# First modulations by single feature tile, with fill matmuls and earlier weight splits, and the last additions behind the products

## The chip, the cores and the metric

The kernel runs on one core of a Trainium2 chip. The metric is the device time of one execution in microseconds (us). The engines are named as in the profile: PE is TensorE's matmul, PEld its weight load, DVE is VectorE, ACT is ScalarE, POOL is GpSimd, SP is SyncE, which issues most transfers. Each engine works through its own queue in the order in which the built program lists it.

## The reference, cut to what matters

Two layers of a diffusion trunk run for 128 context tokens and 256 latent tokens that share all weights, so T = 384 columns. The model width is 1024, that is 8 feature tiles of 128. Each layer is half SwiGLU FFN, token mixing, half FFN, each with RMSNorm and a shift, scale and gate that come from a condition vector:

```python
def _modulation(cond, w, b):
    m = jax.nn.silu(cond) @ w + b
    return jnp.split(m[:, None, :], N_MOD, axis=-1)

def _ada_norm(x, g, shift, scale):
    return _rms(x, g) * (1 + scale) + shift

def _half_ffn(x, shift, scale, gate, g, w1, w3, w2):
    h = _ada_norm(x, g, shift, scale)
    f = (jax.nn.silu(h @ w1) * (h @ w3)) @ w2
    return x + 0.5 * gate * f
```

Nothing can be multiplied in the first FFN before shift and scale of the first sub-layer are known. After the second layer's last FFN only a final RMSNorm follows.

## The kernel before

**Products.** Activations lie with features on the 128 partitions and tokens in columns. Every product is made of three in reduced precision: a value is split into a high part (`hh`, `whi`, cast on ACT, L211) and the rest (`hl`, `wlo`, subtracted on DVE, L212 and L233). `mm3x` (L352 to L354) issues the three: `whi` with `hh`, `whi` with `hl`, `wlo` with `hh`. A *unit* is one of 22 column blocks of `w1` and `w3` of an FFN; it has 8 feature tiles times 2 halves times 3 products = 48 matmuls. The norm's factor is applied after the products, so products can start before the norm is known; its mean is a matmul with ones (L206), whose sum of squares comes from ACT (squares, L200) and POOL (additions, L201).

**The start ("boot").** The modulations of the first sub-layer are computed on PE. The weights come in quarters `q` of two feature tiles each, and each quarter in two halves of 1 MB over the contraction. `sums(q)` multiplies them with the condition (`cs`) in four column strips of 32 of the array, one strip for each pair of shift or scale and feature tile, and DVE copies the result (L954). `apply(q)` transposes it on PE (L958), adds the bias (L960), makes the scale (L123) and the shift's two parts, and then `feed` multiplies x: `hh` on ACT (L232) and `hl` on DVE (L233), each in a context and a latent piece. `begin(ft, ks)` issues the six products of each named feature tile for unit 0 or 1. `load_to` and `split_to` load and split FFN weights (`raw`, `whi`, `wlo`) in the order of a list; three raw buffers and four of each split half are there. PE's order in this block is the order of the code; that of the other engines is chosen by the scheduler. x comes in pairs of feature tiles on the same SP queue.

**The end.** `project_out` computes the second FFN product in four slices `s` of two feature tiles (`m`), and `finish` adds it to x with the gate (L400), takes the square for the next norm and multiplies by the next factor (`feed`). For the last slice of the whole kernel (`apart`) all products of `m` = 0 come before those of `m` = 1, and `finish` of `m` = 0 stands between the two. `Last.finish` (L265) then makes the mean of each token group from two terms, the POOL sum of tiles 0 to 6 and the squares of tile 7, and `put` scales and stores.

Of the kernel before, what the change touches and what calls it, by code (L numbers as in the profile page):

```python
# [43 lines left out]
def trunk(ctx, tc, a):  # L44
# [347 lines left out]
    def project_out(nk, parts, l, v, nxt, name, shared=False, order=None):  # L392
# [14 lines left out]
        for s in range(4):  # L407
            acc = two_banks(f"{name}_acc{s}")
            for k0 in range(0, nk, KD):
# [5 lines left out]
                for m, k in [(m, k) for m in range(2) for k in ks] if apart else [(m, k) for k in ks for m in range(2)]:  # L415
# [5 lines left out]
                    if apart and last:  # L421
                        finish(acc, s, m)
                pump()
            if not apart:
                for m in range(2):
                    finish(acc, s, m)
# [491 lines left out]
    with tc.tile_pool(name="boot", bufs=1) as bp, tc.manual_schedule(engines={mybir.EngineType.PE}):  # L918
        raw_mod, rows = {}, {}

        def load(q):
            nc.sync.dma_start(x[:, 2 * q : 2 * q + 2], a["xT"][:, 2 * q : 2 * q + 2])
            for half in range(2):
                raw_mod[q, half] = bp.tile([P, 4, 512], F32, name=f"raw_mod0_{q}{half}")
                nc.sync.dma_start(raw_mod[q, half], a["modw0"][q, half].rearrange("p (k c) -> p k c", k=4))

        load(0)
        load_to(2)
        for q in range(1, 4):
            load(q)  # L930
        load_to(3)
        units = []

# [10 lines left out]
        def sums(q):  # L944
            acc = one_bank(f"mod0_{q}")[:, :P]
            for half in range(2):
                for k in range(4):
                    for j in range(4):
# [4 lines left out]
            rows[q] = bp.tile([P, P], F32, name=f"modrow0_{q}")  # L953
            dve.tensor_copy(rows[q], acc)  # L954

        def apply(q):
            pt = one_bank(f"modt0_{q}")
            pe.transpose(pt[:, :P], rows[q], ident)  # L958
            for v in range(2):
                dve.tensor_tensor(  # L960
                    mods[0][v][:, 2 * q : 2 * q + 2],
                    pt[:, :P].rearrange("p (v d c) -> p v d c", v=2, d=2)[:, v, :, 0:2],
                    pcol("modb")[:, v * KD + 2 * q : v * KD + 2 * q + 2].unsqueeze(2).broadcast_to([P, 2, 2]),
                    op=ALU.add,
                )
            mod_fix(0, 1, 2 * q, 2 * q + 2)
            feed.shifts(2 * q, 2 * q + 2)
            for d in (2 * q, 2 * q + 1):
                feed.feed(d)
# [183 lines left out]
```

## Time and profile before

| | |
|---|---|
| time, median of 3 runs (lowest to highest) | 1434.32 us (1434.02 to 1434.58) |
| profiled execution: time, span | 1434.01 us, 1432.2 us |
| PE busy, share of the span | 1405.7 us, 98% |
| DVE busy | 1088.3 us, 76% |
| ACT busy | 599.2 us, 42% |
| POOL busy | 123.8 us, 9% |
| bytes moved | 245.26 MB, 171 GB/s over the span |

The span is from the first to the last instruction; the time of the profiled execution is 1.8 us more. Matmuls overlap in their pipeline: one product of 384 columns is listed with 0.34 us, though the next one starts 0.17 or 0.18 us after it, so intervals between starts tell the pace and not the listed length. Idle time of PE is what counts most, and it lies in the first 30 us and the last 15.

### The profile page before, as it was taken

To read this page: it belongs to the slowest core of one execution; us is meant where nothing else is said; L and a number is where in the kernel's file an instruction comes from. 1 tells how busy PE (TensorE), PEld (TensorE's weight loads), DVE (VectorE), ACT (ScalarE), POOL (GpSimd) and SP (SyncE) were. 2 spreads that over 40 slices of the span, in tenths; PEclk is the share of its full clock that TensorE was granted. 3 is DMA by queue.
4 is the path that set the end of the run, shared out by engine and by line. 5 is a ranking of instruction groups with operands and counts; after the bars stand their busy time and mean duration, and the time that the engine had idled before them with its cause. 6 is when DMAs were issued, how large, how long until landed. Compare 5 with 4: busy or idle time off the path is not lost.

```text
span 1432.2 us, 21543 instructions
## 1 busy us (share of the span) xinstructions
PE 1405.7 (98%) x8512; PEld 1367.7 (95%) x8512; DVE 1088.3 (76%) x1829; ACT 599.2 (42%) x981; POOL 123.8 (9%) x97
## 2 busy tenths in 40 slices
PE   6999999999999999999999999999999999999996
PEld 5999999999889999999999999999976999999996
DVE  3899989879876888888869988885687676666433
ACT  4544343435344444343344434333357443444332
POOL 2000000102102000000100000010146200000001
PEclk9999999999999999999999999999999999999999
DMA  9666666563414456656646655665420244333331
GB/s 394 253 215 210 213 198 246 204 223 108 155 45 148 143 195 208 203 178 226 214 162 208 213 209 183 204 213 181 146 89 2 103 141 154 136 130 130 121 103 44
DMA packets 48515, 245.26 MB, mean 171 GB/s; under 512 B 5376, under 2 KB 9856, under 8 KB 29088
## 3 DMA queue, kind: packets, MB, share of 16 engines
q1 hardware_dynamic: 44560, 240.80, 48.3%
q10 hardware_dynamic: 3856, 3.10, 0.7%
q8 instruction: 66, 1.08, 0.3%
q14 instruction: 33, 0.27, 0.1%
HBM read 241.79 MB, written 2.10 MB: 170 GB/s over the span
## 4 chain that ended last, share of the span: by engine, by line
PE 96%; DMA 2%; DVE 1%; ACT 0%; issue 0%; SPq 0%; DVEq 0%; ACTq 0%
PE ffn_p L352 17%; PE ffn_p L354 17%; PE ffn_p L353 17%; PE ffn_acc L345 9%; PE ffn_acc L346 9%; PE ffn_acc L347 9%; DMA raw_mod<-in_modw 2%; PE out_acc L345 2%; PE out_acc L347 2%; PE out_acc L346 2%; PE av L870 1%; PE attn L797 1%; PE attn L352 1%; PE attn L848 1%; PE attn L353 1%; PE attn L354 1%
## 5 line engine op out<-in xcount | busy, mean ns | idle before, releaser
L211 ACT CAST whi<-raw 128x1024 fp32r<-128x1024 f32 (+2 forms) x317 | 324.6, 1027 | 606.5 <-PE ffn_p L353 285.5
L212 DVE TENSOR_TENSOR wlo<-raw,whi 128x1024 fp32r<-128x1024 f32 (+2 forms) x317 | 378.6, 1197 | 164.2 <-ACT whi L211 163.4
L352 PE MATMUL ffn_p<-hh,whi 128*128 128x388 f32 x1408 | 478.4, 340 | 3.0 <-ACT whi L211 3.0
L354 PE MATMUL ffn_p<-hh,wlo 128*128 128x386 f32 x1408 | 475.1, 337 | 0.3 <-DVE wlo L212 0.2
L353 PE MATMUL ffn_p<-hl,whi 128*128 128x384 f32 x1408 | 472.5, 336 | 0.0
L149 DVE SCALAR_TENSOR_TENSOR junk<-modw,cb 128x1024 f32<-128x1024 f32 x256 | 314.4, 1228 | 2.1
L352 PEld LDWEIGHTS ffn_p<-hh,whi 128*128 128x128 f32 x1408 | 265.3, 188 | 4.3 <-ACT whi L211 3.3
L354 PEld LDWEIGHTS ffn_p<-hh,wlo 128*128 128x128 f32 x1408 | 265.9, 189 | 1.5 <-DVE wlo L212 1.5
L353 PEld LDWEIGHTS ffn_p<-hl,whi 128*128 128x128 f32 x1408 | 264.8, 188 | 0.5
L345 PE MATMUL ffn_acc<-gh_ffn,whi 128*128 128x384 f32 x704 | 237.0, 337 | 0.8 <-DVE x L400 0.8
L347 PE MATMUL ffn_acc<-gh_ffn,wlo 128*128 128x384 f32 x704 | 236.9, 337 | 0.0
L346 PE MATMUL ffn_acc<-gl_ffn,whi 128*128 128x384 f32 x704 | 236.9, 336 | 0.0
L201 POOL TENSOR_TENSOR ssq_n<-ssq_n,sq_n 128x384 f32<-128x384 f32 x42 | 59.1, 1408 | 891.6 <-ACT sq_n L200 867.3
L345 PEld LDWEIGHTS ffn_acc<-gh_ffn,whi 128*128 128x128 f32 x704 | 132.8, 189 | 1.2 <-DVE x L400 1.2
L347 PEld LDWEIGHTS ffn_acc<-gh_ffn,wlo 128*128 128x128 f32 x704 | 132.7, 189 | 0.0
L346 PEld LDWEIGHTS ffn_acc<-gl_ffn,whi 128*128 128x128 f32 x704 | 132.7, 189 | 0.0
L438 DVE TENSOR_TENSOR ffn_e<-ffn_p,r_n 128x768 f32<-128x768 f32 x88 | 84.0, 955 | 49.0 <-PE ffn_p L354 48.9
L83 ACT ACTIVATE ffn_e<-ffn_e,ffn_wb 128x128 f32<-128x128 f32 (+1 forms) x176 | 70.2, 448 | 55.3 <-DVE ffn_wb L372 55.0
L212 DVE TENSOR_TENSOR gl_ffn<-ffn_e,gh_ffn 128x384 fp32r<-128x384 f32 x88 | 49.0, 557 | 36.4 <-ACT gh_ffn L211 36.2
L211 ACT CAST gh_ffn<-ffn_e 128x384 fp32r<-128x384 f32 x88 | 44.9, 512 | 58.8 <-DVE ffn_e L442 58.3
L442 DVE SCALAR_TENSOR_TENSOR ffn_e<-ffn_e,ffn_wb 128x128 f32<-128x128 f32 (+1 forms) x176 | 65.0, 412 | 0.0
L233 DVE SCALAR_TENSOR_TENSOR hl<-x,mods,hh 128x128 fp32r<-128x128 f32 (+1 forms) x96 | 57.2, 638 | 2.1 <-ACT hh L232 1.3
(260 smaller groups left out, 1251.5 us busy)
## 6 DMA issues: line engine op xcount, KB each, us to landing
raw<-in_w SPq DMA_DIRECT2D x120, 1024.0 KB, 4.8
modw<-in_modw SPq DMA_DIRECT2D x128, 512.0 KB, 3.4
raw<-in_w SPq DMA_DIRECT2D x16, 768.0 KB, 4.9
raw_mod<-in_modw SPq DMA_DIRECT2D x8, 1024.0 KB, 15.7
raw<-in_w_in SPq DMA_DIRECT2D x8, 1024.0 KB, 5.0
raw<-in_w_out SPq DMA_DIRECT2D x8, 1024.0 KB, 4.9
raw<-in_w_og SPq DMA_DIRECT2D x2, 1024.0 KB, 4.8
raw<-in_w_v SPq DMA_DIRECT2D x2, 1024.0 KB, 4.7
```

What stands on the lines that cost most here:

```text
L83: i = act.activation(out, in_, func, **kw)
L149: i = dve.scalar_tensor_tensor(junk, raw, 1.0, cb[:, c], op0=ALU.mult, op1=ALU.mult, accum_out=mods[l][v][:, d, c : c + 1])
L211: i = act.copy(hi, src).ins
L212: pace["last"] = dve.tensor_tensor(lo, src, f(hi), op=ALU.subtract).ins
L345: first = pe.matmul(out, lhsT=wh, rhs=mh, start=start, stop=False)
L346: pe.matmul(out, lhsT=wh, rhs=ml, start=False, stop=False)
L347: pace["product"] = pe.matmul(out, lhsT=wl, rhs=mh, start=False, stop=stop).ins
L352: first = pe.matmul(out[:, :TX], lhsT=wh, rhs=hh[:, k, :TX], start=(k == 0), stop=False)
L353: pe.matmul(out[:, :T], lhsT=wh, rhs=hl[:, k], start=False, stop=False)
L354: pe.matmul(out[:, :TM], lhsT=wl, rhs=hh[:, k, :TM], start=False, stop=(k == KD - 1))
L438: dve.tensor_tensor(e, pp[:, :, :T], feed.r.unsqueeze(1).broadcast_to([P, 2, T]), op=ALU.mult)
L442: dve.scalar_tensor_tensor(e[:, 1, t0:t1], e[:, 1, t0:t1], wb[:, 1, c : c + 1], e[:, 0, t0:t1], op0=ALU.add, op1=ALU.mult)
```

## The change

The boot block works by single feature tile `d` in place of quarters. The transfer of a tile's modulation weights takes every other run of 128 columns out of the same array in memory, two transfers of 0.5 MB a tile. The four column strips are now shift and scale times the two halves of the contraction, so two strips have to be added after the transpose: per shift or scale one copy and one addition on DVE. `keep(n)` issues `n` matmuls of zeros whose result nobody reads. Weights of unit 0 are split ahead of `apply(0)` in the code. The products of units 0 and 1 follow each tile. In `project_out` the additions of the last slice stand behind all its products.

```diff
-                    if apart and last:
-                        finish(acc, s, m)
                 pump()
-            if not apart:
-                for m in range(2):
-                    finish(acc, s, m)
+            for m in range(2):
+                finish(acc, s, m)
...
-        def load(q):
-            nc.sync.dma_start(x[:, 2 * q : 2 * q + 2], a["xT"][:, 2 * q : 2 * q + 2])
-            for half in range(2):
-                raw_mod[q, half] = bp.tile([P, 4, 512], F32, name=f"raw_mod0_{q}{half}")
-                nc.sync.dma_start(raw_mod[q, half], a["modw0"][q, half].rearrange("p (k c) -> p k c", k=4))
+        still = bp.tile([P, 512], BF16, name="still")
+        pool.memset(still, 0.0)
+
+        def load(d):
+            q, i = divmod(d, 2)
+            if i == 0:
+                nc.sync.dma_start(x[:, d : d + 2], a["xT"][:, d : d + 2])
+            raw_mod[d] = bp.tile([P, 2, 4, 2, P], F32, name=f"raw_mod0_{d}")
+            for h in range(2):
+                nc.sync.dma_start(raw_mod[d][:, h], a["modw0"][q, h].rearrange("p (k v d c) -> p k v d c", k=4, v=2, d=2)[:, :, :, i])
 
         load(0)
+        load_to(1)
+        load(1)
         load_to(2)
-        for q in range(1, 4):
-            load(q)
+        for d in range(2, KD):
+            load(d)
         load_to(3)
...
+        def keep(n):
+
+            pd = one_bank("still")
+            for _ in range(n):
+                pe.matmul(pd, lhsT=still[:, :P], rhs=still, start=True, stop=True)
...
+        def sums(d):
+
+            acc = one_bank(f"mod0_{d}")[:, :P]
+            for k in range(4):
+                for v in range(2):
+                    for h in range(2):
+                        j = 2 * v + h
                         pe.matmul(
-                            acc[32 * j : 32 * j + 32, :], lhsT=cs[:, 4 * half + k, :], rhs=raw_mod[q, half][:, k, j * P : j * P + P],
-                            start=(half == 0 and k == 0), stop=(half == 1 and k == 3), tile_position=(0, 32 * j),
+                            acc[32 * j : 32 * j + 32, :], lhsT=cs[:, 4 * h + k, :], rhs=raw_mod[d][:, h, k, v],
+                            start=(k == 0), stop=(k == 3), tile_position=(0, 32 * j),
                         )
...
+            pt = pt[:, :P].rearrange("p (v h c) -> p v h c", v=2, h=2)
             for v in range(2):
...
+                m = mods[0][v][:, d]
+                dve.tensor_copy(m, pt[:, v, 0, 0:2])
+                dve.scalar_tensor_tensor(m, pt[:, v, 1, 0:2], pcol("modb")[:, v * KD + d : v * KD + d + 1], m, op0=ALU.add, op1=ALU.add)
+            mod_fix(0, 1, d, d + 1)
+            feed.shifts(d, d + 1)
+            feed.feed(d)
+            feed.add(d)
...
+        keep(20)
         sums(0)
+        split_to(1)
         apply(0)
-        split_to(1)
-        begin(0, 0, 1)
-        split_to(2)
-        begin(1, 0, 1)
+        keep(4)
+        begin(0, 0)
         sums(1)
         apply(1)
+        split_to(2)
+        begin(1, 0)
+        begin(0, 1)
         sums(2)
+        begin(1, 1)
+        apply(2)
+        keep(4)
+        sums(3)
...
+        begin(0, 6)
+        apply(7)
+        begin(1, 6)
+        begin(0, 7)
+        begin(1, 7)
         split_to(3)
```

Between `sums(3)` and `begin(0, 6)` the new code repeats one pattern for each tile: `begin(0, d)`, `apply(d + 1)`, `begin(1, d)`, `sums(d + 2)`.

**DVE, first tiles.** DVE's queue before, from the first sum's copy on (`wlo_0` and `wlo_1024` are the two halves of a unit's split weights, the numbers behind them are buffers):

```order
L954 COPY modrow_0_177<-mod_0_144 128x128
L960 TENSOR_TENSOR mods_0_92<-modt_0_179,par 128x4
L960 TENSOR_TENSOR mods_1_93<-modt_0_179,par 128x4
L123 SCALAR_TENSOR_TENSOR mods_1_93<-mods_1_93,par 128x4
L212 TENSOR_TENSOR hh<-mods_0_92,hh 128x2x2
L233 SCALAR_TENSOR_TENSOR hl<-x,mods_1_93,hh 128x128
L233 SCALAR_TENSOR_TENSOR hl<-x,mods_1_93,hh 128x256
L233 SCALAR_TENSOR_TENSOR hl<-x,mods_1_93,hh 128x128
L233 SCALAR_TENSOR_TENSOR hl<-x,mods_1_93,hh 128x256
L212 TENSOR_TENSOR wlo_0_199<-raw_123,whi_0_198 128x1024
L212 TENSOR_TENSOR wlo_1024_203<-raw_123,whi_1024_202 128x1024
```

The same place in the changed program, first tile 0 and then tile 1:

```order
L965 COPY modrow_0_192<-mod_0_175 128x128
L973 COPY mods_0_92<-modt_0_202 128x2
L974 SCALAR_TENSOR_TENSOR mods_0_92<-modt_0_202,par,mods_0_92 128x2
L973 COPY mods_1_93<-modt_0_202 128x2
L974 SCALAR_TENSOR_TENSOR mods_1_93<-modt_0_202,par,mods_1_93 128x2
L212 TENSOR_TENSOR hh<-mods_0_92,hh 128x2
L123 SCALAR_TENSOR_TENSOR mods_1_93<-mods_1_93,par 128x2
L212 TENSOR_TENSOR wlo_0_195<-raw_124,whi_0_194 128x1024
L212 TENSOR_TENSOR wlo_1024_199<-raw_124,whi_1024_198 128x1024
L233 SCALAR_TENSOR_TENSOR hl<-x,mods_1_93,hh 128x128
L233 SCALAR_TENSOR_TENSOR hl<-x,mods_1_93,hh 128x256
```

```order
L965 COPY modrow_1_245<-mod_1_228 128x128
L973 COPY mods_0_92<-modt_1_247 128x2
L974 SCALAR_TENSOR_TENSOR mods_0_92<-modt_1_247,par,mods_0_92 128x2
L973 COPY mods_1_93<-modt_1_247 128x2
L212 TENSOR_TENSOR wlo_0_264<-raw_129,whi_0_263 128x1024
L974 SCALAR_TENSOR_TENSOR mods_1_93<-modt_1_247,par,mods_1_93 128x2
L212 TENSOR_TENSOR hh<-mods_0_92,hh 128x2
L212 TENSOR_TENSOR wlo_1024_268<-raw_129,whi_1024_267 128x1024
L123 SCALAR_TENSOR_TENSOR mods_1_93<-mods_1_93,par 128x2
L233 SCALAR_TENSOR_TENSOR hl<-x,mods_1_93,hh 128x128
L233 SCALAR_TENSOR_TENSOR hl<-x,mods_1_93,hh 128x256
```

Both subtractions of unit 0's weights have moved ahead of tile 0's `hl`, and those of unit 1's weights between tile 1's modulations and its `hl`. Further on the copy of the next tile's sum stands between the two pieces of `hl`, as here in tile 4 (and in the same way in tile 2):

```order
L123 SCALAR_TENSOR_TENSOR mods_1_93<-mods_1_93,par 128x2
L212 TENSOR_TENSOR hh<-mods_0_92,hh 128x2
L233 SCALAR_TENSOR_TENSOR hl<-x,mods_1_93,hh 128x128
L965 COPY modrow_5_441<-mod_5_424 128x128
L233 SCALAR_TENSOR_TENSOR hl<-x,mods_1_93,hh 128x256
L973 COPY mods_0_92<-modt_5_449 128x2
```

**PE, end of the start.** PE's queue where the third unit begins (`ffn_p_206` and `ffn_p_227` are units 0 and 1 of before, `ffn_p_543` is the third unit), before:

```order
L353 MATMUL ffn_p_227<-hl,whi_0_219 128x384
L354 MATMUL ffn_p_227<-hh,wlo_0_220 128x386
L352 MATMUL ffn_p_227<-hh,whi_1024_223 128x388
L353 MATMUL ffn_p_227<-hl,whi_1024_223 128x384
L354 MATMUL ffn_p_227<-hh,wlo_1024_224 128x386
L206 MATMUL mean_n_500<-ssq_n_112,ones 128x384
L352 MATMUL ffn_p_543<-hh,whi_0_480 128x388
```

And now (`ffn_p_221` is unit 0, `ffn_p_271` is unit 1):

```order
L969 MATMUL modt_7_543<-ident,modrow_7_535 128x128
L352 MATMUL ffn_p_271<-hh,whi_0_263 128x388
L353 MATMUL ffn_p_271<-hl,whi_0_263 128x384
L354 MATMUL ffn_p_271<-hh,wlo_0_264 128x386
L352 MATMUL ffn_p_271<-hh,whi_1024_267 128x388
L353 MATMUL ffn_p_271<-hl,whi_1024_267 128x384
L354 MATMUL ffn_p_271<-hh,wlo_1024_268 128x386
L206 MATMUL mean_n_597<-ssq_n_112,ones 128x384
L352 MATMUL ffn_p_221<-hh,whi_0_194 128x388
L353 MATMUL ffn_p_221<-hl,whi_0_194 128x384
```

The norm's mean has moved from behind all products of units 0 and 1 to ahead of the last two groups of six, and the last group of unit 0 now has one group behind it instead of two.

**ACT, the end.** ACT's queue behind the last weights, before (`sq_final` of 128x384 is tile 6, the 128- and 256-column squares are tile 7):

```order
L200 ACTIVATE sq_final_12657<-x 128x384
L256 ACTIVATE x<-x,par 128x384
L250 ACTIVATE sq_final_12681<-x 128x128
L250 ACTIVATE sq_final_12681<-x 128x256
L83 ACTIVATE lnv_final_12692<-mean_final_12686,eps 128x128
L83 ACTIVATE r_final_12695<-lnv_final_12692 128x128
```

And now:

```order
L200 ACTIVATE sq_final_12772<-x 128x384
L250 ACTIVATE sq_final_12778<-x 128x128
L256 ACTIVATE x<-x,par 128x384
L250 ACTIVATE sq_final_12778<-x 128x256
L83 ACTIVATE lnv_final_12789<-mean_final_12783,eps 128x128
L83 ACTIVATE r_final_12792<-lnv_final_12789 128x128
```

The rows of tile 6 stand at the same place in the queue, but the x that they read is written behind the last product; tile 7's first square has moved ahead of the product with `par`.

## Rows read from the trace of the kernel before

**Rows 1.** Busy time by stretches: PE, PEld, DVE, ACT, POOL; clock, DMA share, GB/s.

```profile
20.00:30.00 10.00, 8.19 (x151) 6.73 (x150) 3.92 (x11) 3.58 (x9) 4.67 (x5) 1.00 1.02 424
60.00:100.00 40.00, 40.00 (x232) 40.00 (x231) 37.70 (x63) 16.63 (x25) 0.00 (x0) 1.00 0.67 226
1424.00:1426.00 2.00, 0.00 (x0) 0.00 (x0) 1.90 (x6) 0.00 (x0) 0.00 (x0) 0.98 0.50 152
1426.00:1428.00 2.00, 0.00 (x0) 0.00 (x0) 2.00 (x4) 0.00 (x0) 0.00 (x0) 0.50 0.55 176
```

**Rows 2.** Chain that ended last: start, length in us, what.

```profile
9.97 17.73 DMA raw_mod<-in_modw
```

**Rows 3.** Timeline of PE: start, us, line, operation, count, idle before.

```profile
7.58 1.94 PE L949 MATMUL mod<-raw_mod,cs 128*32 128x128 f32 x32 [7.58 <-DMA raw_mod<-in_modw]
...
15.80 0.69 PE L352 MATMUL ffn_p<-hh,whi 128*128 128x388 f32 x1 [2.98 <-ACT whi L211]
...
18.68 0.53 PE L352 MATMUL ffn_p<-hh,whi 128*128 128x388 f32 x1
19.00 0.52 PE L353 MATMUL ffn_p<-hl,whi 128*128 128x384 f32 x1
...
25.36 1.08 PE L949 MATMUL mod<-raw_mod,cs 128*32 128x128 f32 x32
27.74 1.08 PE L949 MATMUL mod<-raw_mod,cs 128*32 128x128 f32 x32 [1.30 <-DMA raw_mod<-in_modw]
28.75 0.44 PE L352 MATMUL ffn_p<-hh,whi 128*128 128x388 f32 x1
...
35.17 0.45 PE L352 MATMUL ffn_p<-hh,whi 128*128 128x388 f32 x1
...
43.84 0.81 PE L206 MATMUL mean_n<-ssq_n,ones 128*128 128x384 f32 x2
44.19 0.63 PE L352 MATMUL ffn_p<-hh,whi 128*128 128x388 f32 x1
```

**Rows 4.** DMA from 1425.1 to 1426.1 us, the output's first half.

```profile
DMA packets 672, 0.34 MB, mean 336 GB/s; under 512 B 16, under 2 KB 672, under 8 KB 672
```

**Rows 5.** DMA from 1000 to 1030 us: ACT's queue, share of 16 engines.

```profile
q10 hardware_dynamic: 1296, 0.82, 9.5%
```

**Rows 6.** Timeline of ACT and DVE, the same columns.

```profile
14.72 3.87 ACT L211 CAST whi<-raw 128x1024 fp32r<-128x1024 f32 x4
...
24.76 0.29 DVE L954 COPY modrow<-mod 128x128 f32<-128x128 f32 x1 [3.50 <-PE mod L949]
...
25.47 0.23 DVE L960 TENSOR_TENSOR mods<-modt,par 128x4 f32<-128x4 f32 x2 [0.42 <-PE modt L958]
...
26.36 1.58 DVE L233 SCALAR_TENSOR_TENSOR hl<-x,mods,hh 128x128 fp32r<-128x128 f32 x4 [0.31 <-ACT hh L232]
```

**Rows 7.** The page's groups: busy us, mean ns, idle before.

```profile
L212 DVE TENSOR_TENSOR wlo<-raw,whi 128x1024 fp32r<-128x1024 f32 (+2 forms) x317 | 378.6, 1197 | 164.2 <-ACT whi L211 163.4
...
L201 POOL TENSOR_TENSOR ssq_n<-ssq_n,sq_n 128x384 f32<-128x384 f32 x42 | 59.1, 1408 | 891.6 <-ACT sq_n L200 867.3
```

**Rows 8.** Timeline of the end, all engines.

```profile
1415.76 0.34 PE L347 MATMUL ffn_acc<-gh_ffn,wlo 128*128 128x384 f32 x1
1416.14 0.74 DVE L400 SCALAR_TENSOR_TENSOR x<-ffn_acc,mods,x 128x128 f32<-128x128 f32 x2 [10.27 <-PE ffn_acc L347]
...
1416.93 0.44 PE L345 MATMUL ffn_acc<-gh_ffn,whi 128*128 128x384 f32 x1 [0.83 <-DVE x L400]
1416.97 0.52 ACT L200 ACTIVATE sq_final<-x 128x384 f32<-128x384 f32 x1 [11.83 <-DVE x L400]
...
1417.64 1.02 POOL L201 TENSOR_TENSOR ssq_final<-ssq_final,sq_final 128x384 f32<-128x384 f32 x1 [16.77 <-ACT sq_final L200]
...
1420.16 0.82 PE L265 MATMUL mean_final<-ssq_final,ones 128*128 128x128 f32 x4
...
1421.70 0.37 ACT L83 ACTIVATE lnv_final<-mean_final,eps 128x128 f32<-128x128 f32 x1
```

More of the change, by code (lines that the diff above doesn't have):

```diff
@@ L942, in begin @@
                     mm3x(begun[ft][:, i], wh[:, k], wl[:, k], k)
[L944 to L948, printed above, removed]
+        def sums(d):
[4 more added lines that the diff above has]
+                        j = 2 * v + h
                         pe.matmul(
-                            acc[32 * j : 32 * j + 32, :], lhsT=cs[:, 4 * half + k, :], rhs=raw_mod[q, half][:, k, j * P : j * P + P],
-                            start=(half == 0 and k == 0), stop=(half == 1 and k == 3), tile_position=(0, 32 * j),
-                        )
-            rows[q] = bp.tile([P, P], F32, name=f"modrow0_{q}")
-            dve.tensor_copy(rows[q], acc)
@@ L956, in apply @@
-        def apply(q):
-            pt = one_bank(f"modt0_{q}")
-            pe.transpose(pt[:, :P], rows[q], ident)
-            for v in range(2):
[L960 to L969, printed above, removed]
-            for d in (2 * q, 2 * q + 1):
-                feed.add(d)
+                            acc[32 * j : 32 * j + 32, :], lhsT=cs[:, 4 * h + k, :], rhs=raw_mod[d][:, h, k, v],
@@ new lines, in sums, with apply @@
+                            start=(k == 0), stop=(k == 3), tile_position=(0, 32 * j),
+                        )
+            rows[d] = bp.tile([P, P], F32, tag="row", name=f"modrow0_{d}", bufs=3)
+            dve.tensor_copy(rows[d], acc)
+        def apply(d):
+            pt = one_bank(f"modt0_{d}")
+            pe.transpose(pt[:, :P], rows[d], ident)
+            pt = pt[:, :P].rearrange("p (v h c) -> p v h c", v=2, h=2)
+            for v in range(2):
+                m = mods[0][v][:, d]
[5 more added lines that the diff above has]
+            feed.add(d)
@@ L973, in trunk @@
+        keep(20)
         sums(0)
+        split_to(1)
         apply(0)
-        split_to(1)
-        begin(0, 0, 1)
-        split_to(2)
-        begin(1, 0, 1)
+        keep(4)
+        begin(0, 0)
         sums(1)
         apply(1)
+        split_to(2)
+        begin(1, 0)
+        begin(0, 1)
         sums(2)
+        begin(1, 1)
+        apply(2)
+        keep(4)
+        sums(3)
         begin(0, 2)
-        apply(2)
+        apply(3)
+        begin(1, 2)
+        sums(4)
         begin(0, 3)
-        begin(1, 2, 3)
@@ L986, in trunk @@
-        sums(3)
+        apply(4)
+        begin(1, 3)
+        sums(5)
         begin(0, 4)
-        apply(3)
+        apply(5)
+        begin(1, 4)
+        sums(6)
         begin(0, 5)
-        begin(1, 4, 5)
-        begin(0, 6, 7)
-        begin(1, 6, 7)
+        apply(6)
+        begin(1, 5)
+        sums(7)
+        begin(0, 6)
[3 more added lines that the diff above has]
+        begin(1, 7)
         split_to(3)
```

## The prediction

> **What bounds the kernel now.** ("Now" means the kernel before, throughout.) I read the busy time by stretches first: from 60 to 100 us TensorE is busy 40.00 of 40 us [rows 1], so whatever makes it start the steady part later is paid in full at the end. Then the chain that ended last: up to 27.74 us it is made of transfers of modulation weights (`raw_mod`) [rows 2], and from there TensorE carries it. So the first 44 us matter. The timeline of TensorE there [rows 3] shows four sums of modulations and sixteen groups of six products, two units by eight feature tiles. The first sum runs at 7.58, the first product at 15.80; up to 19.00 products follow each other in 0.32 us, a slow pace. Between 35.17 and 43.84 there are 48 products and one transpose in 8.67 us, 0.18 us a product, about 1.06 a group of six. The mean of the norm stands at 43.84, the third unit starts at 44.19, and that is the time to compare. The other end of the kernel comes below.
>
> **The loads.** The eight tile loads carry the 8.4 MB that the eight quarter-and-half loads carry now, but in runs of 512 bytes instead of 8 KB. No load of such runs stands in the trace. Loads of now move 424 GB/s [rows 1]. The nearest row is the output's first half, stored in runs of 512 bytes: 336 GB/s over a microsecond [rows 4]. The far end is the ACT queue's small packets, 1296 with 0.82 MB, on 9.5% of 16 engines for 30 us: 35 ns for 633 bytes, 18 bytes per ns and engine, 288 GB/s for 16 [rows 5]. I take 345, since that microsecond takes in a ramp. The transfers ahead of the first sum hold the same bytes as now (7.58), its megabyte takes 3.0 instead of 2.5 us: 8.1. The stream then brings weights 0 at 10.6, tile 1 at 13.6, weights 1 at 16.1, tile 2 at 20.1, tile 7 at 37.1 (33 at 424 GB/s). On SP's queue the second load of weights moves behind tile 1, and the bytes ahead of it stay the same; all that is behind shifts by the rate alone.
>
> The Trainium skill (DMA: Bandwidth & Descriptors, Specifications) gives 512 B as the smallest transfer at line rate. By it the tiles would come at 424 GB/s and the sum would be 0.6 us lower; the stores [rows 4] do not reach that rate with such runs, so I stay with them.
>
> **TensorE's queue up to the second tile.** The 20 unread products are 512 columns wide against 384: by columns 0.43 us at the slow pace and 0.235 at the fast one. Starting after one memset near 1.3 us, they end near 8.0 if half of them run at the slow pace, about when the first tile is there. If the pace stayed slow they end at 9.9; that 1.8 us is an upper bound. They cost nothing in the first case because TensorE has no data.
> The sum of tile 0 has 32 records, as the half sum at 27.74 has, which gives way to a product after 1.01 us; the first product behind it takes 0.44 instead of 0.34 [rows 3]. So 1.1 us: 9.2. From the copy of a sum to the first operation behind its transpose it is 25.47 - 24.76 = 0.71 [rows 6], with the hand-over 0.75: 9.9. Here the order on DVE and ACT decides. The whole split of weights 0 has moved ahead of tile 0's own multiplication. ACT: shift cast to 10.5, two casts of 0.97 (3.87 for four [rows 6]) behind weights 0, 10.6 to 12.6, then `hh`. DVE: `wlo` twice at 1.2 (the page-wide mean of that group [rows 7]) ends at 14.05, and `hl`, half of 1.58 for four [rows 6], at 14.8. The second product of tile 0 waits for `hl`: 14.8, the last one ends at 15.7. That is when products start now (15.80), but the two tiles of the first quarter are summed by then, here one.
> Sum of tile 1 to 16.8, transposed 17.5. Behind it DVE has three small operations (0.15 each, 0.12 to 0.16 by the two in 0.23 [rows 6]), `wlo`, two small ones, `wlo`, one small one, then `hh` and `hl`: 0.45 + 1.2 + 0.3 + 1.2 + 0.15 = 20.8, and 1.2 more for the first half of `hh` and both of `hl`: 22.0. Before the change nothing stood between these steps: transposed at 25.43, all four `hl` are done by 27.94 [rows 6]. TensorE does unit 1's tile 0 meanwhile and waits. Unit 0's tile 1 ends at 23.0, the sum of tile 2 at 24.1, unit 1's tile 1 at 25.2.
>
> **From 25.2 on the queue itself is the bound.** At 25.36 four tiles are summed now and four groups multiplied; with the change, at 25.2, it is three tiles and four groups. What is left: 4 unread products 0.95; five sums at 1.15 (1.01, and 0.14 for two more changes between kinds of matmul) 5.75; twelve groups 12.7; six transposes 1.2; the mean 0.35: 20.95. On top come waits for `hl`. In tiles 2 and 4 the copy of the next tile's row sits between the two halves of `hl` and waits for that next sum: 0.7 each. In tiles 3, 5 and 6 `hl` comes 2.3 us after the transpose (small operations 0.85, `hh` 0.4, `hl` 0.8, hand-overs), TensorE has 2.2 us between: 0.3 together. Tile 7 has only one group and the mean for cover, 1.4 us: 0.9. Waits 2.6. The third unit would start at 25.2 + 20.95 + 2.6 = 48.75.
> It then waits for its own weights: the cast reuses a buffer that unit 0's last group frees, before the change with two groups of six behind it, in the new order with one, and `lnv` and `r` (ACT) and two `u` (DVE) stand ahead of the split. 0.6 us. So 49.35 against 44.19: **+5.1 us**. The mean's place ahead of the last two groups gains nothing, since DVE and ACT are not waited for behind it [rows 1].
> Bounds: with loads at 424 GB/s +4.5, at 288 +5.6; small operations at 0.06 instead of 0.15 take off 1.0.
>
> **The tail.** Now the second half's first product starts at 1416.93 behind `x L400`, while products come each 0.17 us elsewhere; the one before starts at 1415.76 [rows 8]. Removed: 1.0 us, and 0.1 of the slower first product. Added: the two additions of tile 6 (0.74 [rows 8]) now run behind the last product, and its square and POOL's addition too. From the end E of the products, now at 1420.16: additions start E + 0.2, now `lnv` starts at 1421.70, E + 1.54. Then: additions of tile 6 to 0.94; square 0.09 later, 0.52 long: 1.55; POOL 0.15 later, 1.02 long: 2.72; the mean of group 0 needs this sum, then the rest: 0.05 + 0.25 + 0.53, `lnv` at 3.55. Less 1.54, less 1.1: **+0.9 us**. POOL's spans are rough; with half of it +0.4, with its mean of the whole page, 1.408 us [rows 7], +1.3.
>
> **Sum.** Profiled execution 1434.0 us (span 1432.2 and 1.8 around it) + 5.1 + 0.9 = 1440.0; the median of the runs lies 0.3 above the profiled time: 1440.3.
>
> **The rivals.**
> *The clock does not hold.* The unread products end near 8; then TensorE has a sum, a transpose, four unread products, and until about 25 more pauses than work, one of 2.5 us before tile 0's first product. For it: the sums from 7.58 on did not bring the fast pace now; products at 15.80 still take 0.69 us [rows 3]. Against it: in the tail the granted clock stays at 1.00 (2.4 GHz) to 1424 and 0.98 in 1424 to 1426, and falls to 0.50 (1.2 GHz) only after 1426 [rows 1], though the means began at 1420.16 and `lnv` read them from 1421.70 [rows 8]; no pause in my schedule is as long. Sums and products at the slow pace from 11 to 19.5 cost 2.0 us more, up to 24 4.8: 1442 to 1445.
> *The loads become the bound.* Under about 284 GB/s tile 7 lands after TensorE wants it (41.7): 3.7 us before the stream, 8.2 for the other bytes, 8.4 MB at that rate. At 250 it lands at 45.5 and the sum is 1444. The 288 of [rows 5] is just above.
> *Not slower: only one tile is left behind the last load.* That is what finer tiles can do: if TensorE had worked off its queue when tile 7 lands (33 to 37.1), the rest is its sum 1.1, unit 0 of tile 6 1.06, transpose 0.2, 1.06, mean 0.35, wait 0.9, two groups 2.1, and 0.6 for the weights: 40.4 to 44.5, with the tail 1431.4 to 1435.5. It decides from the point where TensorE is 4.6 us (loads at 345) ahead of my schedule at tile 7, which needs the splits not to hold up tiles 0 and 1. The order speaks against it, since DVE takes its queue in order; the lengths of the small operations on a PSUM source are the soft spot.
>
> **How the numbers follow.** Forecast as summed 0.53; clock 0.15; loads bound 0.08; not slower 0.14; small misses in several terms that bring it below 1437.2 without that case 0.10. About 0.2% (2.9 us) is what a measurement of this kernel tells from no change. The first three are slower: 0.76. Of the not-slower case (1431.4 to 1435.5, the bound is 1431.4) I give 0.04 to faster, 0.01 of the small misses too: faster 0.05, within 0.2% 0.19. The range leaves out the not-slower case and the slowest of the two slow ones: 1436.3 to 1445.3.
>
> **What would show it.** Third unit's first products near 49 instead of 44.19; tile 0's `hl` behind two `wlo` near 14.8; `hl` of tile 1 near 22; TensorE nearly without waits for transfers from 25 us; tiles landing at 336 to 350 GB/s; the tail's `lnv` about 3.5 us after the last product, behind POOL. Wrong, if the waits of TensorE after 25 us are for `raw_mod`, if products run at 0.32 us beyond 20 us, or if the third unit starts by 45.

## The result, and the profile after

The changed kernel takes 1447.06 us (median of 1445.89 to 1448.98) against 1434.34 us (1434.02 to 1434.58) before: a ratio of 1.0091, interval 1.0078 to 1.0104, 12.7 us slower. The forecast was 1440.3 us, between 1436.3 and 1445.3. The sign was right, the size half of what came. The profiled execution is the longest, 1448.98 us with a span of 1447.2; its third unit starts at 55.89 where the forecast had 48.75 (and 44.19 before).

Stretches of the changed kernel, to set beside [rows 1]; columns: stretch, length, TensorE busy (records), granted clock, DMA share, GB/s.

```profile
2.00:7.00 5.00, 5.00 (x14) 1.00 1.00 278
...
13.00:14.00 1.00, 0.00 (x0) 0.76 1.22 298
14.00:20.00 6.00, 4.05 (x34) 0.50 1.04 363
20.00:30.00 10.00, 6.61 (x53) 0.67 1.02 283
24.00:30.00 6.00, 4.65 (x35) 0.50 1.04 295
```

From 20 to 30 us the loads move 283 GB/s instead of 424, and the granted clock falls in 13 to 14 us, while TensorE stands still, and lies at 0.50 (1.2 GHz) in two long stretches. TensorE's timeline at the start, to set beside [rows 3]:

```profile
9.08 1.07 PE L960 MATMUL mod<-raw_mod,cs 128*32 128x128 f32 x30 [0.32 <-DMA raw_mod<-in_modw]
...
10.73 1.03 PE L941 MATMUL still<-still 128*128 128x512 bf16 x4
15.24 0.69 PE L352 MATMUL ffn_p<-hh,whi 128*128 128x388 f32 x1 [3.48 <-ACT hh L232]
16.64 0.69 PE L353 MATMUL ffn_p<-hl,whi 128*128 128x384 f32 x1 [0.71 <-DVE hl L233]
...
18.55 1.93 PE L960 MATMUL mod<-raw_mod,cs 128*32 128x128 f32 x32
20.90 0.33 PE L969 MATMUL modt<-ident,modrow 128*128 128x128 f32 x1 [0.42 <-DVE modrow L965]
...
26.73 0.69 PE L353 MATMUL ffn_p<-hl,whi 128*128 128x384 f32 x1
...
31.67 0.28 PE L969 MATMUL modt<-ident,modrow 128*128 128x128 f32 x1
...
55.89 0.34 PE L352 MATMUL ffn_p<-hh,whi 128*128 128x388 f32 x1
...
56.72 0.44 PE L354 MATMUL ffn_p<-hh,wlo 128*128 128x386 f32 x1 [0.32 <-DVE wlo L212]
```

Behind the unread matmuls 30 of the first sum's 32 records take 1.07 us, the fast pace; then comes a pause of 3.48 us, and the sum of tile 1 takes 1.93 us for its 32 records, the slow one. From 27.22 to 28.18 products follow each other in 0.32 us again: one of the signs of being wrong that the prediction named was products at 0.32 us beyond 20 us. The chain that ended last, its longest pieces up to 26 us (start, length, what):

```profile
2.58 9.89 DMA raw<-in_w
12.49 1.05 ACT whi L211
13.57 0.98 DVE wlo L212
14.71 1.22 DVE wlo L212
15.93 0.67 DVE hl L233 x2
16.64 0.69 PE ffn_p L353
18.62 1.91 PE mod L960 x32
21.75 1.13 DVE wlo L212
23.08 1.13 DVE wlo L212
24.21 0.88 DVE mods L123
25.56 1.13 DVE hl L233 x2
```

Read from the top: the first weights land at 12.47, their splits run, and only then the `hl` of tile 0, though VectorE had its modulations by 11.9 (1.71 us idle ahead of the first `wlo` at 13.57). The same again for tile 1. Where the chain of before was made of loads up to 27.74 [rows 2], it now goes through VectorE's queue. One piece of it is out of scale:

```profile
24.13 0.95 DVE L123 SCALAR_TENSOR_TENSOR mods<-mods,par 128x2 f32<-128x2 f32 x1
```

This operation on two columns takes 0.16 us for every other tile. Here an addition of POOL's (L201) runs from 23.43 for 1.64 us, and `L123` ends at 25.08 as that addition does.

The end of the kernel, to set beside [rows 8]:

```profile
1432.59 0.34 PE L347 MATMUL ffn_acc<-gh_ffn,wlo 128*128 128x384 f32 x1
1432.97 1.39 DVE L400 SCALAR_TENSOR_TENSOR x<-ffn_acc,mods,x 128x128 f32<-128x128 f32 x4 [13.39 <-PE ffn_acc L347]
...
1434.47 1.00 POOL L201 TENSOR_TENSOR ssq_final<-ssq_final,sq_final 128x384 f32<-128x384 f32 x1 [19.89 <-ACT sq_final L200]
...
1436.27 0.37 ACT L83 ACTIVATE lnv_final<-mean_final,eps 128x128 f32<-128x128 f32 x1 [0.93 <-PE mean_final L265]
```

The products end at 1432.76 (the last start and the 0.17 to the next), `lnv` starts 3.51 us later; the forecast had 3.55.

### The profile page after: what moved, and what is told of

Its sections match the earlier page's. It is cut to its first block, busy times and chain, and to the rows that moved or that the text cites. A ratio compares the mean times of both kernels' runs of the same rounds, so it can differ in the third digit from the quotient of the medians.

```text
span 1447.2 us, 21668 instructions
## 1 busy us (share of the span) xinstructions
PE 1421.0 (98%) x8544; PEld 1372.6 (95%) x8544; DVE 1094.5 (76%) x1865; ACT 600.7 (42%) x985; POOL 123.9 (9%) x98
## 4 chain that ended last, share of the span: by engine, by line
PE 95%; DVE 3%; ACT 1%; DMA 1%; issue 0%; SPq 0%; POOLq 0%; DVEq 0%; ACTq 0%
PE ffn_p L352 17%; PE ffn_p L354 17%; PE ffn_p L353 17%; PE ffn_acc L346 8%; PE ffn_acc L347 8%; PE ffn_acc L345 8%; PE out_acc L347 2%; PE out_acc L345 2%; PE out_acc L346 2%; DMA raw<-in_w 1%; PE av L867 1%; PE attn L352 1%; PE attn L794 1%; PE attn L353 1%; PE attn L354 1%; DVE wlo L212 1%
## 5 line engine op out<-in xcount | busy, mean ns | idle before, releaser
L201 POOL TENSOR_TENSOR ssq_n<-ssq_n,sq_n 128x384 f32<-128x384 f32 x42 | 58.6, 1396 | 904.9 <-ACT sq_n L200 903.6
```

## The experiments

"Third unit" is the start of its first product in the run's own profile, to set against 44.19 before and 55.89 in the changed kernel. The last column is the change in time against the changed kernel's 1447.06. Profiles of the same start showed two paces of the same products, 1.6 us apart in all (see e12_again); a median may mix executions of both, so a difference below that is not a price by itself.

| run | what | us | ratio to before (interval) | third unit | to the change |
|---|---|---|---|---|---|
| e1_tail | before, tail edit alone | 1435.23 | 1.0003 (0.9995-1.0012) | 44.31 | |
| e2_start | change without tail edit | 1446.16 | 1.0081 (1.0068-1.0095) | 55.03 | -0.9 |
| e3_fill | change, pauses filled | 1444.73 | 1.0072 (1.0059-1.0084) | 51.19 | -2.3 |
| e4_runs | change, runs of 4 KB | 1445.56 | 1.0080 (1.0066-1.0093) | 53.45 | -1.5 |
| e5_nokeep | change, no unread matmuls | 1446.67 | 1.0086 (1.0072-1.0100) | 53.23 | -0.4 |
| e6_split | change, splits behind feeds | 1443.31 | 1.0064 (1.0051-1.0076) | 50.42 | -3.8 |
| e7_bkeep | before, unread matmuls alone | 1434.20 | 1.0004 (0.9996-1.0013) | 44.21 | |
| e8_combo | tile by tile, all mended | 1436.26 | 1.0014 (1.0005-1.0023) | 45.42 | -10.8 |
| e9_splitfill | e6 with pauses filled | 1441.74 | 1.0052 (1.0038-1.0066) | 49.88 | -5.3 |
| e10_half | before, a sum in two halves | 1434.41 | 1.0002 (0.9993-1.0010) | 43.64 | |
| e11_order | before, other order | 1432.94 | 0.9993 (0.9984-1.0002) | 43.10 | |
| e12_again | the change, unaltered | 1447.65 | 1.0093 (1.0079-1.0107) | 54.37 | +0.6 |

**Which half carries the loss: e1_tail, e2_start.** The first is the kernel before with only the hunk in `project_out`, the second the change with that hunk taken back:

```diff
-                    if apart and last:
-                        finish(acc, s, m)
                 pump()
-            if not apart:
-                for m in range(2):
-                    finish(acc, s, m)
+            for m in range(2):
+                finish(acc, s, m)
```

> The kernel before with only the last additions moved behind both halves' products. Theory: this part costs what the profile of the change showed at the end, about 2.0 us more between the last product and the last Ln, of which about 1.1 us is given back by the first half's additions no longer standing between the two halves: +0.9 us, 1435.2 us (bounds +0.4 to +1.5). Rival A: the wait on the path to the last mean was hidden anyway: +0, 1434.3 us. Rival B: the products without a gap at the second half are worth more than the later additions: -0.5 to -1 us, 1433.5 us.

> The change without its tail, the last additions as before. Theory: the start alone carries the loss, 1447.1 less 0.9 us: 1446.1 us (1445.0 to 1447.5), +11.8 us on the kernel before, with the third unit's first product near 56 us as in the profile of the change. Rival: the loss at the start is partly made good later and the tail carries more than its 0.9 us: under 1445 us.

Alone the tail edit gives +0.8 us on the medians, taken away it gives -0.9: the predicted +0.9 on both sides, though each by itself is within what this measurement tells apart. The start carries the rest, 11.7 us.

**The clock: e3_fill.** Fourteen, eight and five more unread matmuls in the three pauses:

```diff
-        keep(4)
+        keep(18)
         begin(0, 0)
         sums(1)
         apply(1)
         split_to(2)
+        keep(8)
         begin(1, 0)
+        keep(5)
         begin(0, 1)
```

> The change with 27 more unread matmuls in three pauses of TensorE: 14 more ahead of the first product, 8 ahead of the first product of unit 1, 5 ahead of the second tile's products. Theory (the granted clock fell in the pauses and each product behind them took twice its time): the granted clock stays near 1.0 from 13 to 31 us, the pitch of the first unit's products is 0.16 us and not 0.32, the third unit starts 3 to 4 us earlier than 55.9, about 52.5, and the time is 1447.1 - 3.5 = 1443.5 us. Rival A: the fed tiles and the split weights end the waits anyway, so a faster clock only makes the pauses longer: the clock is up, the start of the third unit moves by under 1 us, 1446 to 1447 us. Rival B: the unread matmuls take the place of products: later by up to 2 us, 1449 us.

Stretches and TensorE's timeline of this run:

```profile
14.00:20.00 6.00, 4.78 (x51) 1.00 1.07 358
24.00:30.00 6.00, 5.09 (x79) 1.00 1.13 309
```

```profile
14.98 0.44 PE L353 MATMUL ffn_p<-hl,whi 128*128 128x384 f32 x1 [0.75 <-DVE hl L233]
...
17.55 0.33 PE L969 MATMUL modt<-ident,modrow 128*128 128x128 f32 x1 [0.41 <-DVE modrow L965]
...
23.38 0.45 PE L353 MATMUL ffn_p<-hl,whi 128*128 128x384 f32 x1 [0.31 <-DVE hl L233]
...
26.65 0.27 PE L969 MATMUL modt<-ident,modrow 128*128 128x128 f32 x1
```

The granted clock stays at 1.00, and the transposes of tiles 1 and 2 stand at 17.55 and 26.65 (20.90 and 31.67 in the change; the prediction had the first end at 17.5 and the second start at 25.2). The third unit comes 3.2 us earlier than in e12_again, 4.7 than in the first profile; the medians differ by 2.3 us. So the pauses cost the clock, and the clock some 2 to 3 us, less than the expected 3.5.

**The loads: e4_runs.** The host lays the same weights out tile by tile:

```diff
-a["modw0"][q, h].rearrange("p (k v d c) -> p k v d c", k=4, v=2, d=2)[:, :, :, i]
+a["modw0"][d, h].rearrange("p (k v c) -> p k v c", k=4, v=2)
...
-.transpose(4, 1, 3, 2, 0, 5, 6).reshape(4, 2, P, 2048)
+.transpose(4, 5, 1, 3, 2, 0, 6).reshape(8, 2, P, 1024)
```

> The change with the modulation weights laid out tile by tile, so that each of the two loads of a tile is one run of 4 KB in each partition and not eight of 512 bytes; nothing else is changed. Theory (short runs slow the loads: 283 GB/s at 20 to 30 us and the first weights landed at 12.47 us, against 424 GB/s in the kernel before): rate back to 400 GB/s or more, first weights landed by 10.5 us, the issue of a load by SyncE back to 0.3 to 0.5 us, first product about 1.8 us earlier, third unit 1.5 to 2 us earlier: 1445 us. Rival A: the loads were not what held: 1446.5 to 1447.5 us. Rival B: the first product earlier, but the clock falls in the pauses at other places and gives all of it back: 1446 to 1448 us.

Its stretches, and the start of the first cast of weights on ScalarE:

```profile
12.00:20.00 8.00, 4.58 (x41) 0.79 1.02 416
20.00:30.00 10.00, 8.04 (x51) 0.66 1.02 411
```

```profile
10.18 1.99 ACT L211 CAST whi<-raw 128x1024 fp32r<-128x1024 f32 x2
```

The rate is back at 411 to 416 GB/s, and the first product starts at 12.93. The first weights are cast 2.3 us earlier than in the first profile of the change (10.18 against 12.49), but only 0.9 earlier than in its second, e12_again (11.09). The third unit comes 2.4 and 0.9 us earlier, the median 1.5: as expected, though the runs (1445.15 to 1447.07) overlap those of the change. The clock falls here as it does in e12_again (0.79 from 12 to 20 us, 0.66 from 20 to 30 in both), and against that run the 0.9 us at the cast are still 0.9 at the third unit, so that rival B's loss in slow products does not show.

**What the unread matmuls are worth: e5_nokeep, e7_bkeep.** All three calls of `keep` taken out of the change, and two put into the kernel before:

```diff
+        keep(20)
         sums(0)
         apply(0)
+        keep(4)
         split_to(1)
```

> The change without any of its 28 unread matmuls. Theory (they do not hold the clock where the products run: it was 0.50 at 14 to 20 and 24 to 30 us with them): what is lost is the fast pace of the first sums, which the wait for the first weights hides (landed at 12.47 us), and of the few matmuls at 20 to 24 us; what is won is the third block's 1.0 us ahead of the sums of tile 3. About 1447 us (1446 to 1448.5), equal to the change. Rival A: they are worth 2 us or more, since without them the slow pace lasts over 31 us: 1449 us or above. Rival B: they only stand in the way: 1445 us or below.

> The kernel before with unread matmuls alone: 20 ahead of the first sums, 4 behind the first transpose. Theory: in the kernel before the loads end the waits (third quarter landed at 27.74 us), so a faster clock at 8 to 19 us makes the products of tiles 0 and 1 end up to 3 us earlier and the wait for the third quarter as much longer; the third unit starts at 44.2 us as before and the time is 1434.4 us (within 1 us). Rival A: the chain to the products sets the start: third unit 1 to 3 us earlier, 1432.5 us. Rival B: the 20 end behind the landing of the first quarter and hold up the sums: +0.5 to +1 us.

Neither moves the time: -0.4 and +0.1 us. In the change the fast first sums (1.5 us in all, against 2.5) only lengthen the wait for the first weights, and the clock falls in it. In the kernel before, the first products end 1 us earlier (the second quarter's sum starts at 21.78 against 22.73), and the second half of the third quarter's sum waits for its load until 27.76 as it did until 27.74 [rows 3]: third unit 44.21.

**The split ahead: e6_split, e9_splitfill.** VectorE and ScalarE follow the written order in the start, and the splits stand behind the feeds:

```diff
-tc.manual_schedule(engines={mybir.EngineType.PE})
+tc.manual_schedule(engines={mybir.EngineType.PE, mybir.EngineType.DVE, mybir.EngineType.Activation})
...
         sums(0)
-        split_to(1)
         apply(0)
+        split_to(1)
         keep(4)
         begin(0, 0)
         sums(1)
         apply(1)
         split_to(2)
-        begin(1, 0)
         begin(0, 1)
+        begin(1, 0)
```

The second kernel has `keep(14)` for this `keep(4)` and a `keep(8)` behind `split_to(2)` as well.

> The change with VectorE and ScalarE in written order in the start, the splits of both units' weights behind the feed of tiles 0 and 1, and the second tile's products of unit 0 ahead of the first tile's products of unit 1. Theory (split ahead, VectorE's rest of tile 0 stands behind weights that land at 12.47 us and are ready at 15.85): rest of tile 0 done by 13 us, first product near 13.8 instead of 15.2, rest of tile 1 done near 22.5 instead of 26.7, third unit 2 to 3 us earlier, 1444.5 us (1443.5 to 1446). Rival A: the weights' own pieces end the wait either way: within 0.7 us of the change, 1446.5 to 1447.5 us. Rival B: with longer pauses the clock stays low for longer and takes back what is won.

> The kernel with the splits behind the feeds (1443.3 us), and on top unread matmuls that fill its two long pauses: 10 more ahead of the first product, 8 behind the transpose of tile 1. Theory (clock and split order each hold up the start by themselves): the products at 13.5 to 24.7 us, 18 of them at 0.32 us, come at 0.17, the third unit 2 to 3 us earlier than in that kernel, 1440.5 to 1441.5 us. Rival A: with the splits out of the way the chain from transpose to feed ends each wait, the faster clock only lengthens the pauses: 1442.5 to 1443.5 us. Rival B: the added matmuls hold up the products: above 1444 us.

VectorE in e6_split:

```profile
11.73 0.88 DVE L233 SCALAR_TENSOR_TENSOR hl<-x,mods,hh 128x128 fp32r<-128x128 f32 x2 [0.40 <-ACT hh L232]
13.47 2.36 DVE L212 TENSOR_TENSOR wlo<-raw,whi 128x1024 fp32r<-128x1024 f32 x2 [0.86 <-ACT whi L211]
18.30 0.29 DVE L965 COPY modrow<-mod 128x128 f32<-128x128 f32 x1 [2.47 <-PE mod L960]
...
20.42 0.88 DVE L233 SCALAR_TENSOR_TENSOR hl<-x,mods,hh 128x128 fp32r<-128x128 f32 x2 [0.40 <-ACT hh L232]
```

`hl` of tile 0 is done at 12.6 and of tile 1 at 21.3, against 16.6 and 26.7. From the row copy to the end of `hl` it is 3.0 us for tile 1, against 6.1 in the change (20.55 to 26.68). From the end of tile 1's transpose to the first product with its `hl` it is 2.4 us here and 5.5 in the change; without the splits in between, `L123` also comes clear of POOL's addition (0.16 us). The third unit starts at 50.42, behind the mean again as before the change, 4.0 us earlier than in e12_again. This is the largest single part, 3.8 us, a little more than the theory's range. The edit does three things (written order of two engines, splits behind the feeds, two groups of products swapped), and no run takes them apart. The clock is low here too (0.72 at 14 to 20 us, 0.55 at 21 to 24), and the filling takes it to 1.00 and another 1.6 us: less than the 2 to 3 expected. In the two profiled executions (1442.03 and 1441.60 us) the third unit moves by only 0.5 us: with the clock up, TensorE waits for `wlo` four times up to 23.70, 1.9 us in all. The faster clock lengthens the pauses, as rival A had it, but it is the split weights that end them and not the feed. The profiled execution of e6_split is its fastest, with a mean granted clock of 0.996 against 0.991 or 0.992 in the other four.

**Can tile by tile win: e8_combo.** Loads of 4 KB runs, splits behind the feeds, each next tile's sum ahead of a tile's products, 20, 12 and 6 unread matmuls, the old tail:

```diff
         sums(0)
-        split_to(1)
         apply(0)
-        keep(4)
+        split_to(1)
+        keep(12)
+        sums(1)
         begin(0, 0)
-        sums(1)
         apply(1)
         split_to(2)
+        keep(6)
+        begin(0, 1)
+        sums(2)
         begin(1, 0)
-        begin(0, 1)
-        sums(2)
+        apply(2)
         begin(1, 1)
-        apply(2)
-        keep(4)
         sums(3)
...
```

> Tile by tile with what the runs so far showed taken together: loads in 4 KB runs, splits behind the feeds, sums of tile d+1 ahead of the products of tile d, unread matmuls long enough to fill the pauses (20, 12, 6), last additions as before the change. Theory: the loads of the tiles end near 32 us and TensorE has some 25 us of work from 13 us on, so the third unit starts at 39 to 42 us against 44.2 before: 1430 to 1433 us, faster than both kernels. Rival A: the chain of each tile from transpose to rest, about 3.5 us, still shows at every tile: third unit near 46 us, 1436 us. Rival B: the loads, not the order, set it: third unit near 43 us, 1433.5 us.

TensorE in this run, the stretch and the rows behind it:

```profile
24.00:42.00 18.00, 17.69 (x213) 1.00 1.02 416
```

```profile
27.08 1.08 PE L963 MATMUL mod<-raw_mod,cs 128*32 128x128 f32 x32
28.09 0.44 PE L352 MATMUL ffn_p<-hh,whi 128*128 128x388 f32 x1
...
30.71 1.08 PE L963 MATMUL mod<-raw_mod,cs 128*32 128x128 f32 x32
...
42.49 0.44 PE L352 MATMUL ffn_p<-hh,whi 128*128 128x388 f32 x1 [0.80 <-ACT hh L232]
```

10.8 of the 12.7 us are back, but it does not beat the kernel before: 1436.26, third unit at 45.42. From 24 to 42 us TensorE is busy 17.69 of 18 us, so no load and no split holds it up there; the sums of one tile and the next stand 3.63 us apart. Before, two tiles took 6.42 us from 28.75 to 35.17 [rows 3], 3.21 each. Over eight tiles that is 3.4 us more of TensorE's own time, by estimate. Of the 3.63, the sum takes 1.01 (27.08 to the product at 28.09) and twelve products at 0.176 take 2.11, so 0.5 goes into the changes between sum, products and transpose; the first product behind the sum, for one, is followed after 0.37 us. Before, the same count leaves 0.31 for two tiles (6.42 less 4.22 for 24 products and 1.89 for the sum, from 33.28 to the product at 35.17), since a quarter has these changes once for two. The theory had counted products and sums alone. Rival A's figures came, third unit near 46 and 1436 us, but not by its mechanism: from 24 us on the chain behind the transpose shows at the last tile alone, as the 0.80 us at 42.49.

**The kernel before, in another order: e10_half, e11_order.** e10_half puts the six products of `begin(0, 2)` between the two halves of `sums(2)`. e11_order loads unit 1's weights behind the second quarter and has this order:

```diff
-        sums(2)
+        sums(2, (0,))
         begin(0, 2)
+        sums(2, (1,))
         apply(2)
```

```diff
+        keep(20)
         sums(0)
         apply(0)
         split_to(1)
+        keep(12)
         begin(0, 0, 1)
-        split_to(2)
-        begin(1, 0, 1)
         sums(1)
         apply(1)
-        sums(2)
-        begin(0, 2)
+        split_to(2)
+        keep(4)
+        begin(0, 2, 3)
+        sums(2, (0,))
+        begin(1, 0, 1)
+        sums(2, (1,))
+        begin(1, 2)
         apply(2)
-        begin(0, 3)
-        begin(1, 2, 3)
-        sums(3)
+        begin(1, 3)
+        sums(3, (0,))
         begin(0, 4)
+        sums(3, (1,))
+        begin(0, 5)
         apply(3)
...
```

> The kernel before with its third sum in two parts, six products of the second quarter between them, where TensorE waited 1.30 us for the second half of the third quarter. Theory: the products fill the pause, everything behind comes 1.0 us earlier: 1433.3 us. Rival: the fourth quarter's load, which lands near 33 us, takes the place of the wait: 1434.2 us.

> The kernel before (quarters, long runs, last additions as before) with unread matmuls (20, 12, 4), the second unit's weights loaded behind the second quarter and not ahead of it, and its products used as cover for the third and fourth quarter's loads. Theory (the loads bound the start up to 27.7 us, the chain behind each sum the rest): second quarter 2.5 us earlier, 48 products done when the third quarter's second half lands, third unit at 41 to 42.5 us: 1431.5 to 1432.5 us. Rival A: the later weights of unit 1 hold up ScalarE and VectorE where the feeds of the second and third quarter are due: third unit at 44 to 45, 1434 to 1435 us. Rival B: gain at the start but the third unit's own weights late: 1433 us.

e10_half moves the third unit by 0.55 us and nothing that the times show. e11_order moves it by 1.1 us and the median to 1432.94 us, 1.2 us below the 1434.16 of the kernel before beside it. That is under both kernels' medians, but its interval (0.9984 to 1.0002) still holds no change.

**The same kernel again: e12_again.**

> The changed kernel once more, unaltered, for a second profile. Its runs so far lie in two groups, 1446.0 and 1448.4 us; the profiled one, of the upper group, took 16.91 us for 96 products of the first feed-forward part, the same start with the old tail took 16.75. Theory (the upper group is this slower pace over some 150 us, about 1.5 us): a run near 1446 shows 16.75, a run near 1448.5 shows 16.91. Rival: the two groups come from the clock at the start, and the pace of these products has nothing to do with them.

Stretches from 60 to 210 us, first of the changed kernel, then of e2_start, whose start is the same; both are products of the first feed-forward part without a gap:

```profile
60.00:210.00 150.00, 150.00 (x853) 1.00 0.63 218
```

```profile
60.00:210.00 150.00, 150.00 (x861) 1.00 0.62 217
```

The kernel before has 862 in this stretch, e12_again 854. Nine products fewer, at 0.174 us, are 1.6 us, spread evenly; from 500 to 650 us all have 862. The changed kernel's profile, e12_again's and e3_fill's show this, the other eleven do not. The profiled run of e12_again took 1447.46 us and shows it, so with e2_start (1445.70, plus 0.9 for its tail, without it) the theory fits, though no profile shows a run of the changed kernel near 1446 us. What sets the pace stays open.

The two profiles of the changed kernel have this pace in common and still lie 1.52 us apart (1448.98 and 1447.46). All of that is there when the third unit starts (55.89 and 54.37), and 1.4 of it when the first weights are cast (12.49 and 11.09). TensorE in e12_again:

```profile
15.23 0.55 PE L353 MATMUL ffn_p<-hl,whi 128*128 128x384 f32 x1 [0.96 <-DVE hl L233]
...
19.35 0.33 PE L969 MATMUL modt<-ident,modrow 128*128 128x128 f32 x1 [0.41 <-DVE modrow L965]
...
25.19 0.69 PE L353 MATMUL ffn_p<-hl,whi 128*128 128x384 f32 x1
...
30.17 0.27 PE L969 MATMUL modt<-ident,modrow 128*128 128x128 f32 x1
```

## Why the prediction was right and wrong

**Right: the sign, and both bounds named.** The start became TensorE's and VectorE's instead of the loads'. From the transpose of tile 2 on the prediction had 24.15 us to the third unit's work, wait for weights included; the profile has 24.69 (31.67 to 56.36, its start and 0.47 us of late weights). The tail's +0.9 us came as summed (e1_tail, e2_start), and behind POOL as said. The tiles' loads never became the bound, though they moved at 283 GB/s, just under the 284 of that rival: TensorE came to them 7 us later than forecast.

**Wrong: the forecast term "TensorE's queue up to the second tile", +6.5 us at the third transpose (31.67 against 25.2).** Its pieces, in us, beside the same ones in the second profile of the change and in the run that held the clock:

| piece | forecast | change | e12_again | e3_fill |
|---|---|---|---|---|
| second product of tile 0 starts | 14.8 | 16.64 | 15.23 | 14.98 |
| from there to the end of tile 1's transpose | 2.7 | 4.59 | 4.45 | 2.90 |
| from there to the first product with tile 1's `hl` | 4.5 | 5.50 | 5.51 | 5.50 |
| from there to the start of tile 2's transpose | 3.2 | 4.94 | 4.98 | 3.27 |
| tile 2's transpose starts | 25.2 | 31.67 | 30.17 | 26.65 |

- Mostly the slow pace, the second and fourth piece: 1.9 and 1.7 us. The step that failed is "no pause in my schedule is as long": the schedule had a pause of 2.5 us ahead of the first product, and the clock fell in 13 to 14 us, within the real one of 3.48 us, then once more behind the waits for `wlo`. In e12_again the pause was 2.54 us, as scheduled, with one of 0.96 behind the next product, and the clock fell all the same (0.79 from 12 to 20 us). The rival was named and priced at 2.0 to 4.8, at a chance of 0.15; its 1442 to 1445 still falls short of 1447, since the other pieces came on top. e3_fill shows it by holding the clock: the two pieces shrink to 2.90 and 3.27, close to the forecast. Of the 3.5 us that it is ahead of e12_again at tile 2's transpose, 3.2 are left at the third unit and 2.3 in the medians (2.7 between the two profiled executions); where the rest goes is not shown.
- Loads, 1.8 us in the first profile and 0.4 in the second. The step "I take 345" (GB/s) failed: the loads moved 283 at 20 to 30 us (304 in e12_again). The lower bound of [rows 5], 288, was nearer than the stores of [rows 4]. At the first weights this cost much in one execution alone: they landed at 12.47 there and not at 10.6, but by 11.1 in e12_again. Why the same kernel's loads land 1.4 us apart stays open. That 512 bytes suffice for the line rate, as the Trainium skill (DMA: Bandwidth & Descriptors, Specifications) has it, these runs do not bear out: the same bytes in 4 KB runs moved at 411 to 416.
- The chain from the transpose of tile 1 to its `hl`, 1.0 us. The order on VectorE was read rightly, and the mis-sized term is the last small operation: 0.15 in the forecast, 0.95 measured, while POOL's addition ran. In e3_fill `L123` takes 0.96 and the piece the same 5.50; in e5_nokeep, where no addition runs at that time, they take 0.16 and 4.8.

Together these are the 6.5, but for rounding, and 5.0 in e12_again. From the transpose on 0.5 us is added, which makes 7.0 at the third unit; the slower pace of the first feed-forward part, which no step of the prediction had, adds 1.6. With the sum's 1440.0 that is 1448.6, against 1448.98 measured in this execution; the median lies 1.9 lower.

**The price of the change's own parts** is another account, by undoing one at a time: split ahead 3.8 us, pauses at the slow clock 2.3, short runs 1.5, tail 0.9, unread matmuls 0.4 (the last three are within the spread of the runs and the 1.6 us between the two paces). They overlap: e9_splitfill undoes two worth 6.1 us and gets 5.3.

**The rival "not slower: only one tile is left behind the last load"** asked for splits that hold up neither tile 0 nor tile 1. With these (e8_combo) the third unit starts at 45.42, still outside its 40.4 to 44.5: TensorE's own 3.63 us a tile takes the place of the load. The rival's price assumed that TensorE could have worked off its queue by the last landing; at that pace it can't.

## What to carry to other kernels

Smaller pieces do not shorten the serial chain behind each piece (here 3 us from the copied row to `hl`), they only halve the work that covers it: before cutting finer, count what TensorE has to do under each chain and what each cut costs in its own queue. Splitting weights ahead puts an engine that takes its queue in order behind a load; let it first finish what it already has the data for. Unread matmuls as filler that holds the clock were worth something here only where they covered every pause up to the steady stream, and little where a load or a split, and not TensorE's pace, ended the next wait. And one execution's early loads are no sure measure: the same kernel had them 1.4 us apart.

## What the runs showed of the hardware

- Loads in 512-byte runs (steps of 1 KB) moved 283 GB/s from 20 to 30 us in the first profile of the change and 303 or 304 in the six others that have them there; the same bytes in 4 KB runs moved 411 (e4_runs) and 415 (e8_combo), in 8 KB runs 424 [rows 1]. They also held up SyncE's queue. SyncE's issue of the weight load behind the first tile, in the changed kernel and then in e4_runs (1.97 to 2.35 us in the six others; behind the second tile 4.89 in the changed kernel, 3.88 to 4.08 in the others and 0.33 in e4_runs):

```profile
2.58 3.01 SPq L317 DMA_DIRECT2D raw<-in_w  x1
```

```profile
2.11 0.43 SPq L317 DMA_DIRECT2D raw<-in_w  x1
```

- The granted clock's column tells nothing before its first rise. In e5_nokeep, without unread matmuls, it reads 1.00 where the products come at the slow pace, 0.32 us apart:

```profile
14.00:20.00 6.00, 4.53 (x38) 1.00 1.07 356
```

```profile
16.57 0.53 PE L352 MATMUL ffn_p<-hh,whi 128*128 128x388 f32 x1
16.90 0.52 PE L353 MATMUL ffn_p<-hl,whi 128*128 128x384 f32 x1
```

- An operation of VectorE on two columns (`L123`) that takes 0.16 us took 0.95 to 0.98 where it began while POOL's addition `L201` ran (the changed kernel, e2_start, e3_fill, e4_runs, e12_again), and ended with that addition, to within 0.03 us. That the addition held it up is read from these times alone; no run changes POOL's work.
- One stream of products, with no wait in it and the clock at 1.00, ran at two paces in different executions of the same start: 8.37 or 8.45 us for 48 products, for some 160 us and in the first feed-forward part alone.
